# Whole-row merges in generic slots, and a later start of the first layer's second modulation

## The chip, the cores and the metric

The kernel runs on one core of a Trainium2 chip. A core has five engines that run side by side, each its instructions in order: PE (TensorE, matrix products into PSUM), DVE (VectorE), ACT (ScalarE), POOL (GpSimd) and SP (SyncE), which here issues nearly all DMA transfers. The metric is the device time of one launch in microseconds (us). Times of before: 2560.27, 2557.42 and 2563.41, median 2560.27.

## The reference

Two layers of a hybrid block over 512 tokens of x and 256 of ctx, 1024 features, in fp32. Layer 0 updates both; layer 1 only x, so it works on 512 columns where layer 0 works on 768.

```python
sh1, sc1, g1, sh2, sc2, g2 = split(silu(c) @ w_mod[l] + b_mod[l], 6)   # "modulation", from c and from c_ctx
u = x * (1 + sc1) + sh1
a, qkv, o_pre, g_if, cq, ckv, kr, gates = split(u @ w_in + b_in)
y_a = silu(layer_norm(depthwise_conv31(val * sigmoid(gate)))) @ w_conv_out
y_b = (sigmoid(o_pre) * head_norm(bidirectional_mlstm(...))) @ w_ml_out
y_c = softmax_attention(...) @ w_mla_out
g_a, g_b, g_c = split(sigmoid(gates), 3)
y = (g_a * y_a + g_b * y_b + g_c * y_c) @ w_out + b_out          # the merge
x = layer_norm(alpha * x + g1 * y)
x = layer_norm(alpha * x + g2 * (relu(u2 @ w1 + b1)**2 @ w2 + b2))
```

## The kernel before, in words

Everything is kept with features on the 128 partitions and tokens along the free axis. A feature tile of layer 0 is 128x768 (512 tokens of x, then 256 of ctx), one of layer 1 uses 512 columns of it. fp32 precision comes from splitting each operand into a high and a low part: every product is three matmuls (L266 hi by hi, L267, L268), and each weight block of 128x1024 is loaded as `wr` (L258, 512 KB), cast to `wh` on ACT (L261) and subtracted to `wl` on DVE or POOL (L262). There are three buffers each of wr, wh and wl, and `wget` loads LOOK = 2 blocks ahead. So a load of wr waits until the subtraction of the block three before it is done, and the cast into wh waits for the last matmul that reads the block three before it.

A scheduler places the instructions: from the program's order, priorities and pools it makes one fixed order per engine. All DMAs that matter stand in one order on SP. If a transfer there waits for something, all behind it wait too.

The stages of a layer that the change touches, in order:

- The modulation. The shares that are needed first (sh1, sc1) are made at the start. The others, two parts r of four groups each in layer 0, come from the generator `mod_pieces`: for each group eight loads `wm` (L160, 256 KB), each multiplied on DVE into two running sums `mda` (L163 for the first, L165 for the others), then eight small matmuls that gather the sums (L173), a copy on ACT (L176), a transpose (L178) and an addition of the bias on DVE (L181). `pull(k)` takes k steps of that generator; a step is one wm with its two operations. 64 steps make all of it. In layer 1 these pulls find nothing left.
- The 24 gates (`gate`, L760): three rows b of eight tiles mt; a gemm of 48 matmuls in layer 0, tanh on ACT, and a store of the tile to `z_dram` (L779). Behind gate 10 the convolution's normalization runs (`ln_fm` with `conv_emit`: L314 to L336, L770 to L774). Each gate pulls 2. Then four output gates `ot` (L791), also with `pull(2)`.
- `ht` (L816 to L819, then a split into `hth` on ACT, L272, and `htl` on DVE, L273): the mLSTM's heads, input of the second merge.
- `merge(b, ...)` for b = 0 (w_co, the convolution) and b = 1 (w_mo, the mLSTM): eight gemms `ps` of four k-blocks each, two for each weight block. For each gemm the row z_dram[b, mt] is loaded back as `ml` (L76), multiplied with the result on DVE (L803), for b = 1 added to the row of b = 0 on POOL (L806), and stored again (L807). PSUM has two buffers `pg` for gemms, so the third gemm needs the first one's L803.
- The last merge (L1057 on, w_ao): the same with two rows loaded (L1065, L1066 on DVE), whose result is split into `zp` (cast on ACT, L1067, subtraction on DVE, L1068) as input of w_out.

Before, a row of 768 columns is handled in pieces: 512 + 256 in the first two merges, three times 256 (two in layer 1) in the last, each piece an `ml` tile of 128x512 out of the pool "m", whose eight buffers it shares with wm, mda, th, y, xr and others. The pool "gen" has 35 slots of 128x768 for everything else.

Of the kernel before, what the change touches and what calls it, by code (L numbers as in the profile page):

```python
# [9 lines left out]
F32 = mybir.dt.float32  # L10
F32R = mybir.dt.float32r
AF = mybir.ActivationFunctionType
OP = mybir.AluOpType
# [31 lines left out]
def build(tc, I, out):  # L45
    nc = tc.nc
# [1 line left out]
    ctx = ExitStack()  # L48
    cp = ctx.enter_context(tc.tile_pool(name="const", bufs=1))
    wp = ctx.enter_context(tc.tile_pool(name="w", bufs=3))  # L50
    gp = ctx.enter_context(tc.tile_pool(name="gen", bufs=35))
    vp = ctx.enter_context(tc.tile_pool(name="v", bufs=12))
    mp = ctx.enter_context(tc.tile_pool(name="mw", bufs=8))
    sp = ctx.enter_context(tc.tile_pool(name="small", bufs=6))
# [17 lines left out]

    def mload(src):
        n = src.shape[1]
        t = mp.tile([128, 512], F32, name="ml", tag="m")
        nc.sync.dma_start(t[:, :n], src)  # L76
        return t[:, :n]

# [200 lines left out]
    def gemm(w, koff, nk, act, spec):  # L279


        ps = pg()
        if isinstance(spec, int):
            spec = [(0, 512, 0), (512, spec, 512)][:1 + (spec > 512)]
        for c0, c1, o in spec:
            for k in range(nk):
                a, b = (koff + k) * 128, (koff + k + 1) * 128
                mark[0] = mm3(ps[:, o:o + c1 - c0], w[0][:, a:b], w[1][:, a:b], act[k][0][:, c0:c1],
                              act[k][1][:, c0:c1], k == 0, k == nk - 1)
        return ps  # L290
# [55 lines left out]
    def pull(k):  # L346
        for _ in range(k):
            next(mods, None)
# [104 lines left out]
    for l in range(L):  # L453
# [322 lines left out]
        for b in range(3):  # L776
            for mt in range(8):
                g = gate(b, mt)
                nc.sync.dma_start(z_dram[b, mt, :, :n], g[:, :n])  # L779
                some_taps(3)  # L780
                pull(2)
                if b * 8 + mt == 10:
                    some_taps(200)
                    ln_fm(ca, 4, groups, conv_emit)
# [3 lines left out]
        for h in range(MH):  # L788
            ps = win(MT_O + h, n)
            t = slot("ot")  # L790
            A.activation(t[:, :n], ps[:, :n], AF.Tanh, bias=HB(MT_O + h), scale=0.5)  # L791
            ot.append(t)
            pull(2)

        def merge(b, wname, act):
            for mp2 in range(4):
                w = wget(wname, l, mp2)
                for i in range(2):
                    mt = 2 * mp2 + i
                    ps = gemm(w, 4 * i, 4, act, n)  # L800
                    for c0, c1 in segs:
                        g = mload(z_dram[b, mt, :, c0:c1])
                        V.scalar_tensor_tensor(g, g, 1.0, ps[:, c0:c1], op0=OP.add, op1=OP.mult)  # L803
                        if b:
                            z0 = mload(z_dram[b - 1, mt, :, c0:c1])
                            G.tensor_tensor(g, g, z0, op=OP.add)  # L806
                        nc.sync.dma_start(z_dram[b, mt, :, c0:c1], g)  # L807
                    pull(2)


# [246 lines left out]
        for mp2 in range(4):  # L1057
            w = wget("w_ao", l, mp2)
            for i in range(2):
                mt = 2 * mp2 + i  # L1060
                ps = gemm(w, 4 * i, 4, oT, n)
                for (_, _, c0, c1), zz in zip(tg_, zg):
                    g = mload(z_dram[2, mt, :, c0:c1])
                    z0 = mload(z_dram[1, mt, :, c0:c1])
                    V.scalar_tensor_tensor(g, g, 1.0, ps[:, c0:c1], op0=OP.add, op1=OP.mult)  # L1065
                    V.tensor_tensor(g, g, z0, op=OP.add)  # L1066
                    A.copy(zz[mt][0], g)  # L1067
                    V.tensor_sub(zz[mt][1], g, zz[mt][0])  # L1068

        parts = [(0, 0, S), (1, S, T)][:len(groups)]  # L1070
        acc = [None] * 8
# [222 lines left out]
```

## Time and profile before

| | |
|---|---|
| median of three runs | 2560.27 us |
| profiled execution: its own time | 2557.35 us |
| its span | 2555.5 us, 1.85 outside of it |
| mean granted TensorE clock | 0.993 |
| SP issues `ml<-z_dram` | 104 of 128 KB (2.8 us to landing), 48 of 256 KB (4.4 us) |
| `z_dram<-ml` | 32 of 256 KB (4.5 us) and smaller |
| `wm<-w_mod` | 192 of 256 KB (4.5 us) |

A profile's page has the busy time of each engine, the chain of work that ended last, and groups of instructions by line; the trace gives each instruction's start. A window's row gives for a stretch of the span the busy time of each engine with its instructions in brackets, the granted clock, the DMA engines' share and what they moved. A row of the timeline is start, duration, engine, line, operation, tiles, and in square brackets the idle time before it with what ended it. "SPq" rows are DMA issues.

### The profile page before, as it was taken

The numbers are of one execution on the slowest core, as the hardware profiler recorded it, in microseconds if no ns is written. First come the engines' busy times: TensorE is split into PE (matmuls) and PEld (weight loads), VectorE is DVE, ScalarE is ACT, GpSimd is POOL, SyncE is SP. The second block draws the span as 40 slices with busy tenths as digits, with TensorE's granted clock in tenths as the row PEclk, the third lists the DMA queues.
The fourth block names the chain that finished last, engine by engine and source line by source line (L and its number), as shares of the span: only waits on it lengthen the run. The fifth ranks groups of instructions, "written<-read, shape, count | busy, mean of one in ns | idle before, by whom it ended". The sixth has DMA issues, their size and how long they took to land.

```text
span 2555.5 us, 38339 instructions
## 1 busy us (share of the span) xinstructions
PE 2470.4 (97%) x15272; PEld 2163.8 (85%) x15272; DVE 1580.6 (62%) x2847; ACT 939.5 (37%) x1607; POOL 298.7 (12%) x235
## 2 busy tenths in 40 slices
PE   7899989999999999999999999999999999999997
PEld 5888878888888899888888888977888888888887
DVE  4999976363356777655554379996043567554456
ACT  3123323222457563222222253333324575432323
POOL 0002132203000021000000031023411001100002
PEclk9999999999999999999999999999999999999999
DMA  7122344466110654343342252233563106333333
GB/s 264 53 75 70 98 163 161 166 195 210 62 34 1 188 168 142 122 131 115 108 129 88 65 149 78 59 106 101 175 203 111 50 18 213 101 99 92 99 94 113
DMA packets 137235, 298.45 MB, mean 117 GB/s; under 512 B 13776, under 2 KB 55248, under 8 KB 137056
## 3 DMA queue, kind: packets, MB, share of 16 engines
q1 hardware_dynamic: 137056, 296.00, 36.9%
q8 instruction: 120, 1.97, 0.3%
q14 instruction: 59, 0.48, 0.1%
HBM read 265.49 MB, written 30.46 MB: 116 GB/s over the span
## 4 chain that ended last, share of the span: by engine, by line
PE 81%; DVE 9%; DMA 4%; ACT 2%; issue 2%; POOL 1%; SPq 0%; DVEq 0%; ACTq 0%; POOLq 0%
PE pg L266 21%; PE pg L267 21%; PE pg L268 21%; PE pt L1003 2%; PE pt L982 2%; PE pt L266 2%; PE pt L267 2%; PE pt L268 2%; DVE ca L494 2%; DMA wm<-w_mod 1%; DMA ml<-z_dram 1%; PE pg L536 1%; PE pg L538 1%; PE pg L537 1%; DVE st L315 1%
## 5 line engine op out<-in xcount | busy, mean ns | idle before, releaser
L261 ACT CAST wh<-wr 128x1024 fp32r<-128x1024 f32 (+1 forms) x328 | 345.6, 1055 | 1202.4 <-PE pg L267 825.5
L262 DVE TENSOR_TENSOR wl<-wr,wh 128x1024 fp32r<-128x1024 f32 (+2 forms) x272 | 338.6, 1246 | 410.1 <-ACT wh L261 406.3
L268 PE MATMUL pg<-uh,wl 128*128 128x512 f32 (+1 forms) x1280 | 456.3, 356 | 2.2 <-DVE wl L262 2.2
L266 PE MATMUL pg<-uh,wh 128*128 128x512 f32 (+1 forms) x1280 | 457.2, 357 | 1.2 <-ACT gt__17278 L760 1.2
L267 PE MATMUL pg<-ul,wh 128*128 128x512 f32 (+1 forms) x1280 | 455.5, 356 | 0.7 <-POOL ul L1171 0.6
L266 PE MATMUL pg<-hidh,wh 128*128 128x512 f32 (+1 forms) x832 | 285.4, 344 | 3.9 <-DVE mv L318 2.0
L267 PE MATMUL pg<-hidl,wh 128*128 128x512 f32 (+1 forms) x832 | 284.9, 342 | 0.0
L268 PE MATMUL pg<-hidh,wl 128*128 128x512 f32 (+1 forms) x832 | 284.2, 342 | 0.0
L266 PEld LDWEIGHTS pg<-uh,wh 128*128 128x128 f32 x1280 | 244.2, 191 | 35.4 <-issue 2.5
L268 PEld LDWEIGHTS pg<-uh,wl 128*128 128x128 f32 x1280 | 243.9, 191 | 34.4 <-DVE wl L262 2.7
L267 PEld LDWEIGHTS pg<-ul,wh 128*128 128x128 f32 x1280 | 244.1, 191 | 33.2 <-POOL ul L1171 1.0
L494 DVE SCALAR_TENSOR_TENSOR ca<-hc,cols,ca 128x511 f32<-128x511 f32 (+9 forms) x360 | 227.8, 673 | 2.4
L262 POOL TENSOR_TENSOR wl<-wr,wh 128x1024 fp32r<-128x1024 f32 x56 | 145.7, 2602 | 562.6 <-ACT wh L261 562.6
L267 PE MATMUL pg<-u2l,wh 128*128 128x512 f32 (+1 forms) x608 | 210.3, 347 | 0.3 <-POOL u2l L1082 0.2
L1139 DVE SCALAR_TENSOR_TENSOR acc<-pg,mod,acc 128x512 f32<-128x512 f32 (+1 forms) x168 | 106.0, 659 | 168.6 <-PE pg L268 168.6
L268 PE MATMUL pg<-u2h,wl 128*128 128x512 f32 (+1 forms) x608 | 210.1, 347 | 0.0
L266 PE MATMUL pg<-u2h,wh 128*128 128x512 f32 (+1 forms) x608 | 209.9, 347 | 0.0
L165 DVE SCALAR_TENSOR_TENSOR mda<-wm,sil,mda 128x512 f32<-128x512 f32 x224 | 176.2, 808 | 7.6 <-DMA wm<-w_mod 5.0
L266 PEld LDWEIGHTS pg<-hidh,wh 128*128 128x128 f32 x832 | 157.3, 190 | 25.3 <-issue 3.5
L321 POOL TENSOR_TENSOR rs<-rs,mhalf 128x1 f32<-128x1 f32 x30 | 24.4, 819 | 1298.5 <-DVE rs L320 1298.5
L267 PEld LDWEIGHTS pg<-hidl,wh 128*128 128x128 f32 x832 | 157.9, 190 | 18.7 <-DVE hidl L1129 1.6
L268 PEld LDWEIGHTS pg<-hidh,wl 128*128 128x128 f32 x832 | 157.7, 189 | 18.0
(359 smaller groups left out, 4754.1 us busy)
## 6 DMA issues: line engine op xcount, KB each, us to landing
wr<-w SPq DMA_DIRECT2D x140, 512.0 KB, 3.6
wr<-w_in_fm SPq DMA_DIRECT2D x104, 512.0 KB, 3.8
wm<-w_mod SPq DMA_DIRECT2D x192, 256.0 KB, 4.5
wr<-w_out SPq DMA_DIRECT2D x40, 512.0 KB, 3.9
ml<-z_dram SPq DMA_DIRECT2D x104, 128.0 KB, 2.8
ml<-z_dram SPq DMA_DIRECT2D x48, 256.0 KB, 4.4
z_dram<-ml SPq DMA_DIRECT2D x32, 256.0 KB, 4.5
dm<-m_dram SPq DMA_DIRECT2D x20, 256.0 KB, 4.4
```

The source lines that it names most:

```text
L165: ins = V.scalar_tensor_tensor(av[v], w, sil[:, k, v:v + 1], av[v], op0=OP.mult, op1=OP.add)
L261: A.copy(h[:, :n], r[:, :n])
L262: eng.tensor_sub(lo[:, :n], r[:, :n], h[:, :n])
L266: PE.matmul(ps, hs, xh, start=first, stop=False)
L267: PE.matmul(ps, hs, xl, start=False, stop=False)
L268: return PE.matmul(ps, ls, xh, start=False, stop=last)
L315: V.bn_stats(st[:, hf * 6:(hf + 1) * 6], ps)
L494: V.scalar_tensor_tensor(acc[:, a:b], h[:, a + d:b + d], wd(15 + d), acc[:, a:b], op0=OP.mult, op1=OP.add)
L536: PE.matmul(o, uh[:, t0:t0 + 128], wh[:, a:b], start=(k == 0), stop=False)
L982: PE.transpose(p2[:, y * 128:(y + 1) * 128], P[:, (k4 + y) * 128:(k4 + y + 1) * 128], ident)
L1003: PE.matmul(po[64 * i:64 * i + 64, :256], va[B_.k0 + k][:, h * 64:h * 64 + 64], B_.pts[i][k // 2][:, k % 2, :], start=(k == 0), stop=(k == ...
L1139: V.scalar_tensor_tensor(acc[mt][:, c0:c1], ps[:, c0:c1], mc[:, 40 + mt, v:v + 1], acc[mt][:, c0:c1], op0=OP.mult, op1=OP.add)
```

## The change

Four things. `mload` takes a generic slot of 128x768 instead of a tile of pool "m", and there are 40 such slots for 35; `dynamic_dma_scratch_size=1024` frees the room. The merges load, multiply, add and store whole rows; only the cast and subtraction of the last merge (now L1067 and L1068 behind L1064 and L1065) still go by groups. Gates 0 to 7 pull nothing, the others 3 steps, and so do the output gates.

```diff
--- before.py
+++ after.py
@@ -48,7 +48,7 @@
     ctx = ExitStack()
     cp = ctx.enter_context(tc.tile_pool(name="const", bufs=1))
     wp = ctx.enter_context(tc.tile_pool(name="w", bufs=3))
-    gp = ctx.enter_context(tc.tile_pool(name="gen", bufs=35))
+    gp = ctx.enter_context(tc.tile_pool(name="gen", bufs=40))
     vp = ctx.enter_context(tc.tile_pool(name="v", bufs=12))
     mp = ctx.enter_context(tc.tile_pool(name="mw", bufs=8))
     sp = ctx.enter_context(tc.tile_pool(name="small", bufs=6))
@@ -72,7 +72,7 @@
 
     def mload(src):
         n = src.shape[1]
-        t = mp.tile([128, 512], F32, name="ml", tag="m")
+        t = slot("ml")
         nc.sync.dma_start(t[:, :n], src)
         return t[:, :n]
 
@@ -778,7 +778,8 @@
                 g = gate(b, mt)
                 nc.sync.dma_start(z_dram[b, mt, :, :n], g[:, :n])
                 some_taps(3)
-                pull(2)
+                if b:
+                    pull(3)
                 if b * 8 + mt == 10:
                     some_taps(200)
                     ln_fm(ca, 4, groups, conv_emit)
@@ -790,7 +791,7 @@
             t = slot("ot")
             A.activation(t[:, :n], ps[:, :n], AF.Tanh, bias=HB(MT_O + h), scale=0.5)
             ot.append(t)
-            pull(2)
+            pull(3)
 
         def merge(b, wname, act):
             for mp2 in range(4):
@@ -798,13 +799,12 @@
                 for i in range(2):
                     mt = 2 * mp2 + i
                     ps = gemm(w, 4 * i, 4, act, n)
-                    for c0, c1 in segs:
-                        g = mload(z_dram[b, mt, :, c0:c1])
-                        V.scalar_tensor_tensor(g, g, 1.0, ps[:, c0:c1], op0=OP.add, op1=OP.mult)
-                        if b:
-                            z0 = mload(z_dram[b - 1, mt, :, c0:c1])
-                            G.tensor_tensor(g, g, z0, op=OP.add)
-                        nc.sync.dma_start(z_dram[b, mt, :, c0:c1], g)
+                    g = mload(z_dram[b, mt, :, :n])
+                    V.scalar_tensor_tensor(g, g, 1.0, ps[:, :n], op0=OP.add, op1=OP.mult)
+                    if b:
+                        z0 = mload(z_dram[b - 1, mt, :, :n])
+                        G.tensor_tensor(g, g, z0, op=OP.add)
+                    nc.sync.dma_start(z_dram[b, mt, :, :n], g)
                     pull(2)
 
 
@@ -1059,13 +1059,13 @@
             for i in range(2):
                 mt = 2 * mp2 + i
                 ps = gemm(w, 4 * i, 4, oT, n)
+                g = mload(z_dram[2, mt, :, :n])
+                z0 = mload(z_dram[1, mt, :, :n])
+                V.scalar_tensor_tensor(g, g, 1.0, ps[:, :n], op0=OP.add, op1=OP.mult)
+                V.tensor_tensor(g, g, z0, op=OP.add)
                 for (_, _, c0, c1), zz in zip(tg_, zg):
-                    g = mload(z_dram[2, mt, :, c0:c1])
-                    z0 = mload(z_dram[1, mt, :, c0:c1])
-                    V.scalar_tensor_tensor(g, g, 1.0, ps[:, c0:c1], op0=OP.add, op1=OP.mult)
-                    V.tensor_tensor(g, g, z0, op=OP.add)
-                    A.copy(zz[mt][0], g)
-                    V.tensor_sub(zz[mt][1], g, zz[mt][0])
+                    A.copy(zz[mt][0], g[:, c0:c1])
+                    V.tensor_sub(zz[mt][1], g[:, c0:c1], zz[mt][0])
 
         parts = [(0, 0, S), (1, S, T)][:len(groups)]
         acc = [None] * 8
@@ -1284,7 +1284,7 @@
     from concourse.bass_utils import run_bass_kernel_spmd
 
     arrays = pack(inputs)
-    nc = bacc.Bacc("TRN2", target_bir_lowering=False, num_devices=1)
+    nc = bacc.Bacc("TRN2", target_bir_lowering=False, num_devices=1, dynamic_dma_scratch_size=1024)
     aps = {k: nc.dram_tensor(k, v.shape, F32, kind="ExternalInput").ap() for k, v in arrays.items()}
     out = nc.dram_tensor("out", (S, D), F32, kind="ExternalOutput").ap()
     with tile.TileContext(nc) as tc:
```

The order changes at three places that matter below. Names carry a running number; the same tile has other numbers before and now.

TensorE in layer 0's gates, where the first modulation group is gathered. Before, this stands eight matmuls into gate pg_3241:

```order
L268 MATMUL pg_3241<-uh_178,wl_3094 128x512
L266 MATMUL pg_3241<-uh_264,wh_3093 128x512
L267 MATMUL pg_3241<-ul_265,wh_3093 128x512
L173 MATMUL pt_3067<-mda_2777,pick_86 32x128 [waits DVE_49]
L173 MATMUL pt_3067<-mda_2777,pick_86 32x128 x3
L268 MATMUL pg_3241<-uh_264,wl_3094 128x512
L173 MATMUL pt_3067<-mda_2778,pick_86 32x128 [waits DVE_49]
L173 MATMUL pt_3067<-mda_2778,pick_86 32x128 x3
L266 MATMUL pg_3241<-uh_272,wh_3093 128x512
```

Now the first group stands in gate pg_3645, four gates later, just ahead of the convolution's normalization (L314):

```order
L268 MATMUL pg_3645<-uh_178,wl_3300 128x512
L266 MATMUL pg_3645<-uh_264,wh_3299 128x512
L267 MATMUL pg_3645<-ul_265,wh_3299 128x512
L173 MATMUL pt_3433<-mda_3283,pick_86 32x128 [waits DVE_49]
L173 MATMUL pt_3433<-mda_3283,pick_86 32x128 x3
L173 MATMUL pt_3433<-mda_3284,pick_86 32x128 x4
L268 MATMUL pg_3645<-uh_264,wl_3300 128x512
L266 MATMUL pg_3645<-uh_272,wh_3299 128x512
L178 MATMUL pt_3444<-cst_78,modrows_3442 128x128 [waits Activation_49]
L314 MATMUL pt_3454<-cst_78,ca_606 128x128
```

The group's sums and their wait are the same; 192 matmuls of gates 7 to 10 now stand ahead of them.

SP in layer 1, where the rows of the first merge are loaded. Before, among the gates' stores and weights (w_in_fm), long ahead of the weights w_co and w_mo:

```order
L258 DMA wr_17383<-w_in_fm 128x1024 [waits DMAHW6_49,DMAHW1_49,Pool_49]
L76 DMA ml_17888<-z_dram_104 128x512 [waits DVE_49,PE_49]
L76 DMA ml_17905<-z_dram_104 128x512 [waits DMAHW0_49,DVE_49]
L76 DMA ml_17928<-z_dram_104 128x512 [waits DVE_49,PE_49]
L76 DMA ml_17945<-z_dram_104 128x512 [waits DMAHW2_49,DVE_49,PE_49]
L76 DMA ml_17968<-z_dram_104 128x512 [waits DMAHW3_49,DVE_49]
L779 DMA z_dram_104<-gt__17278 128x512 [waits DMAHW4_49,Activation_49]
L779 DMA z_dram_104<-gt__17312 128x512 [waits DMAHW5_49,Activation_49]
```

Now behind the third w_mo block, at the merge itself:

```order
L258 DMA wr_17725<-w_co 128x1024 [waits DMAHW5_49,DVE_49]
L258 DMA wr_17765<-w_mo 128x1024 [waits DMAHW7_49,DMAHW2_49,DVE_49]
L258 DMA wr_17805<-w_mo 128x1024 [waits DMAHW0_49,DVE_49]
L258 DMA wr_17845<-w_mo 128x1024 [waits DMAHW4_49,DMAHW1_49,DVE_49]
L76 DMA ml_17704<-z_dram_104 128x512 [waits PE_49]
L76 DMA ml_17721<-z_dram_104 128x512 [waits DMAHW6_49]
L76 DMA ml_17744<-z_dram_104 128x512 [waits PE_49]
L76 DMA ml_17761<-z_dram_104 128x512 [waits DVE_49]
L76 DMA ml_17784<-z_dram_104 128x512 [waits DVE_49]
L807 DMA z_dram_104<-ml_17704 128x512 [waits DMAHW5_49,DMAHW2_49,DVE_49]
```

wr_17845 waits for DVE, for the subtraction wl_17728 of the last w_co block, whose buffer it takes. The row loads moved behind it. In layer 0 the rows ml_5016 and on stand behind the third w_mo block in the same way. VectorE of layer 1 there, before:

```order
L262 TENSOR_TENSOR wl_17872<-wr_17869,wh_17871 128x1024 [waits DMAHW0_49,PE_49,Activation_49]
L819 TENSOR_SCALAR ht_17821<-ht_17821,cols1_83 128x512 [waits DVE_49]
L803 SCALAR_TENSOR_TENSOR ml_17888<-ml_17888,pg_17875 128x512 [waits PE_49]
L273 TENSOR_TENSOR htl_17830<-ht_17821,hth_17829 128x512 [waits DMAHW6_49,Activation_49]
L818 SCALAR_TENSOR_TENSOR ht_17833<-ot_17753,pt_17834 128x512
L819 TENSOR_SCALAR ht_17833<-ht_17833,cols1_83 128x512 [waits DVE_49]
L803 SCALAR_TENSOR_TENSOR ml_17905<-ml_17905,pg_17892 128x512 [waits PE_49]
L262 TENSOR_TENSOR wl_17912<-wr_17909,wh_17911 128x1024 [waits DMAHW1_49,Activation_49]
L273 TENSOR_TENSOR htl_17842<-ht_17833,hth_17841 128x512 [waits DMAHW4_49,Activation_49]
```

And now:

```order
L262 TENSOR_TENSOR wl_17728<-wr_17725,wh_17727 128x1024 [waits DMAHW1_49,PE_49,Activation_49]
L273 TENSOR_TENSOR htl_17658<-ht_17649,hth_17657 128x512 [waits DMAHW2_49,Activation_49]
L818 SCALAR_TENSOR_TENSOR ht_17661<-ot_17602,pt_17662 128x512 [waits DMAHW4_49]
L819 TENSOR_SCALAR ht_17661<-ht_17661,cols1_83 128x512 [waits DVE_49]
L273 TENSOR_TENSOR htl_17670<-ht_17661,hth_17669 128x512 [waits Activation_49]
L818 SCALAR_TENSOR_TENSOR ht_17673<-ot_17635,pt_17674 128x512 [waits DMAHW2_49]
L819 TENSOR_SCALAR ht_17673<-ht_17673,cols1_83 128x512 [waits DVE_49]
L273 TENSOR_TENSOR htl_17682<-ht_17673,hth_17681 128x512 [waits DMAHW6_49,Activation_49]
L803 SCALAR_TENSOR_TENSOR ml_17704<-ml_17704,pg_17691 128x512 [waits DMAHW5_49]
L803 SCALAR_TENSOR_TENSOR ml_17721<-ml_17721,pg_17708 128x512 [waits DMAHW6_49]
```

All of ht now stands ahead of the first L803 (ml_17704).

SP in layer 1's last merge, before, round one of its w_out loads:

```order
L76 DMA ml_20278<-z_dram_104 128x256 [waits DMAHW5_49,DVE_49]
L76 DMA ml_20284<-z_dram_104 128x256 [waits DMAHW4_49,DVE_49]
L76 DMA ml_20286<-z_dram_104 128x256 [waits DVE_49]
L76 DMA ml_20305<-z_dram_104 128x256 [waits DMAHW7_49,DMAHW6_49,DVE_49]
L76 DMA ml_20307<-z_dram_104 128x256 [waits DMAHW1_49,DVE_49]
L258 DMA wr_20469<-w_out 128x1024 [waits DMAHW0_49,DVE_49]
L76 DMA ml_20313<-z_dram_104 128x256 [waits DVE_49]
L76 DMA ml_20315<-z_dram_104 128x256 [waits DMAHW2_49,DVE_49]
```

And now:

```order
L76 DMA ml_20051<-z_dram_104 128x512 [waits DMAHW4_49]
L76 DMA ml_20053<-z_dram_104 128x512 [waits DMAHW5_49]
L258 DMA wr_20237<-w_out 128x1024 [waits DMAHW6_49,DVE_49]
L76 DMA ml_20080<-z_dram_104 128x512 [waits DMAHW7_49]
L76 DMA ml_20082<-z_dram_104 128x512 [waits DMAHW0_49]
L76 DMA ml_20103<-z_dram_104 128x512 [waits DMAHW1_49]
L76 DMA ml_20105<-z_dram_104 128x512 [waits DMAHW2_49]
L258 DMA wr_20269<-w_out 128x1024 [waits DMAHW3_49,DVE_49]
L76 DMA ml_20132<-z_dram_104 128x512 [waits DMAHW4_49]
L76 DMA ml_20134<-z_dram_104 128x512 [waits DMAHW5_49]
L258 DMA wr_20301<-w_out 128x1024 [waits DMAHW6_49,DVE_49]
L76 DMA ml_20155<-z_dram_104 128x512 [waits DMAHW7_49]
```

Before, seven pairs of pieces stand ahead of that w_out load, wr_20469, the first of three; now four row loads, those of mt 0 and 1, stand ahead of the first of them, wr_20237, and those of mt 2 and 3 (ml_20080 to ml_20105), of mt 4, and of mt 5 to 7 follow one w_out load each. Each of these waits for DVE, for a subtraction.

## The prediction

> **What bounds the kernel now.** I read the page first: the busy shares, and the chain of waits that ended last.
>
> ```profile
> PE 2470.4 (97%) x15272; PEld 2163.8 (85%) x15272; DVE 1580.6 (62%) x2847; ACT 939.5 (37%) x1607; POOL 298.7 (12%) x235
> PE 81%; DVE 9%; DMA 4%; ACT 2%; issue 2%; POOL 1%; SPq 0%; DVEq 0%; ACTq 0%; POOLq 0%
> L165 DVE SCALAR_TENSOR_TENSOR mda<-wm,sil,mda 128x512 f32<-128x512 f32 x224 | 176.2, 808 | 7.6 <-DMA wm<-w_mod 5.0
> ```
>
> TensorE carries the time, so an edit matters only where TensorE stops. Next I took windows round the places that the change touches (after the length: PE busy, weight loads, DVE, ACT, POOL, granted clock, DMA share, GB/s), what TensorE waited for there, and the chain from 300 to 420.
>
> ```profile
> 320.00:330.00 10.00, 9.36 (x53) 7.89 (x51) 8.18 (x20) 2.84 (x4) 6.10 (x4) 1.00 0.48 150
> 330.00:340.00 10.00, 2.66 (x19) 1.37 (x20) 9.12 (x15) 0.27 (x1) 0.99 (x1) 0.72 0.57 177
> 340.00:350.00 10.00, 10.00 (x55) 8.63 (x54) 9.29 (x16) 1.85 (x2) 2.11 (x1) 0.94 0.63 207
> ...
> 600.00:610.00 10.00, 8.09 (x43) 6.79 (x42) 4.32 (x7) 0.00 (x0) 6.23 (x5) 1.00 0.87 268
> 1670.00:1680.00 10.00, 5.98 (x26) 5.04 (x25) 9.04 (x11) 1.06 (x2) 2.37 (x1) 0.83 0.43 125
> 1880.00:1890.00 10.00, 10.00 (x46) 8.29 (x45) 8.06 (x13) 3.11 (x4) 0.00 (x0) 1.00 0.74 238
> ```
> ```profile
> PE pt L173 <- DVE mda L165: 8.0, 1, 8.0
> ```
> ```profile
> PE pg L266 <- DVE ml L803: 3.6, 2, 1.9
> PE pt L173 <- DVE mda L165: 0.6, 1, 0.6
> ```
> ```profile
> PE pg L266 <- DVE ml L1065: 1.4, 2, 1.2
> ```
> ```profile
> 328.44 2.89 DVE hacc L748 x3
> ...
> 337.34 0.65 PE pt L173 x8
> 337.99 0.73 PE pg L268
> 338.72 0.58 PE pt L173 x8
> 339.31 0.72 PE pg L266
> ...
> 355.14 0.57 PE pt L173 x16
> ...
> 373.91 2.85 DVE mda L165
> ```
>
> The wait rows (total, times, longest) are of 320 to 345, of 540 to 612 (layer 0's merges) and of 2104 to 2140 (layer 1's w_ao merge). At 329 TensorE reaches the transposes of the first modulation group (L173), while VectorE still has that group's sums behind the normalization (L748): a stop of 8.0 us. In layer 1's first merge (1880 to 1890) TensorE never stops.
>
> **What the change gains.** (1) Gates 0 to 7 pull nothing, so the first group's transposes stand four gates later, behind 192 more matmuls, which are four gates of 8.3 us, 33 us in all. Its last five weight loads now stand on SP behind the store of gate 8, which by gates of 8.3 us ends at 345 (the wait at 329 is eight matmuls into gate 7). The first lands 4.4 us on (256 KB, row below), the others 0.98 apart at the 268 GB/s of 600 to 610, and six sums of 0.81 follow the last: 359. TensorE comes to the transposes at 329 + 33 = 362. So the 8.0 us go, and the slow stretch behind them: 0.65 + 0.73 + 0.58 + 0.72 = 2.68 us for what takes 0.57 (16 transposes at 355) and two matmuls of 0.23, so 1.65 too much, and some 0.5 at clock 0.94. That is 10.1; I leave 0.1 for what stays: **-10.0** (between 0, if the wait moves along, and -10.6). What hides the sums then is gate matmuls; without that cover they cost the 8.0 again.
> (2) The sum at 373.91 stood ahead of the conv normalization's statistics, 2.85 us; in the new order none stands there: **-2.4**, the part that TensorE stopped (0 to -2.9). The later groups come 17 to 25 us apart and need 14 x 0.81 = 11.3 us of VectorE: hidden. The one behind the normalization waits about 2 us now and then: 0.
> (3) VectorE loses 63 instructions and SP 88 issues. Covered by TensorE's matmuls, since VectorE is 62% busy: 0. The scratch setting and the five slots issue nothing: 0.
>
> **What it costs: row loads come to stand behind weight loads on SP.** Layer 1's first merge, as it runs now, has the durations:
>
> ```profile
> 1878.35 1.05 ACT L261 CAST wh<-wr 128x1024 fp32r<-128x1024 f32 x1 [2.08 <-PE pg L267]
> ...
> 1882.89 0.62 ACT L272 CAST hth<-ht 128x512 fp32r<-128x512 f32 x1 [2.96 <-DVE ht L819]
> ```
> ```profile
> 1879.43 1.23 DVE L262 TENSOR_TENSOR wl<-wr,wh 128x1024 fp32r<-128x1024 f32 x1 [0.22 <-ACT wh L261]
> 1880.58 0.69 DVE L273 TENSOR_TENSOR htl<-ht,hth 128x512 fp32r<-128x512 f32 x1
> 1881.18 0.68 DVE L818 SCALAR_TENSOR_TENSOR ht<-ot,pt 128x512 f32<-128x512 f32 x1
> 1881.78 0.68 DVE L803 SCALAR_TENSOR_TENSOR ml<-ml,pg 128x512 f32<-128x512 f32 x1
> 1882.38 0.48 DVE L819 TENSOR_SCALAR ht<-ht,cols 128x512 f32<-128x512 f32 x1
> ...
> 1894.85 0.69 DVE L803 SCALAR_TENSOR_TENSOR ml<-ml,pg 128x512 f32<-128x512 f32 x1 [2.03 <-PE pg L268]
> ```
> ```profile
> 571.17 1.02 DVE L803 SCALAR_TENSOR_TENSOR ml<-ml,pg 128x512 f32<-128x512 f32 x2 [3.16 <-PE pg L268]
> ```
> ```profile
> 1786.65 2.54 SPq L76 DMA_DIRECT2D ml<-z_dram  x5
> ...
> 1880.69 0.33 SPq L258 DMA_DIRECT2D wr<-w_mo  x1
> ```
> ```profile
> ml<-z_dram SPq DMA_DIRECT2D x104, 128.0 KB, 2.8
> ml<-z_dram SPq DMA_DIRECT2D x48, 256.0 KB, 4.4
> ```
>
> A gemm takes 2.03 + 0.69 = 2.7 us in layer 1 and 3.16 + 1.02 = 4.2 in layer 0. Today the rows are loaded from 1786 on, some 90 us early. In the new order they stand behind the w_mo load of 1880.69. That one waits until the subtraction of 1879.43 has freed its slot, and the cast ahead of it waits for the end of the second gemm (1878.35). So the first row is issued at 1881.1 and lands at about 1885 (4 us; 4.4 by the group). VectorE's order also puts every L818, L819 and L273 ahead of the first L803: from 1880.6 on, 0.6 each from start to start, L273, L818, L819, the cast on ACT, L273, L818, L819, the cast, L273, to 1885.9, then L803 to 1886.6. The third gemm needs the PSUM buffer that this L803 frees (there are two), and TensorE is in order. It stands from 1878.4 to 1886.6: **+8.2** (4, if only the load counts; 9, if it lands late).
>
> Layer 0's first merge has the same order with rows of 768 columns. I take 0.95 us for an operation on a whole row, since its two parts take 1.02 at 571. After the second gemm: cast 1.05, subtraction 1.15, then L273 0.9, L818 0.95, small ones and L819 1.15, cast 0.85, L273 0.95, L803 0.95, together 7.95; TensorE has 0.7 of transposes meanwhile. With a little waiting for the load, 7.5. The 3.6 + 0.6 = 4.2 us of the wait rows go, 1.9 of them in the second merge, whose rows are then loaded five gemms ahead: **+3.3** (0 to +6).
>
> The merges of w_ao (L1057 on), layer 1 as it runs now:
>
> ```profile
> 2102.13 9.29 SPq L76 DMA_DIRECT2D ml<-z_dram  x10
> 2112.09 0.33 SPq L258 DMA_DIRECT2D wr<-w_out  x1
> ...
> 2117.06 0.33 SPq L258 DMA_DIRECT2D wr<-w_out  x1
> ...
> 2124.16 0.33 SPq L258 DMA_DIRECT2D wr<-w_out  x1
> ```
> ```profile
> 2109.28 1.06 ACT L261 CAST wh<-wr 128x1024 fp32r<-128x1024 f32 x1 [0.63 <-PE pg L267]
> ```
> ```profile
> 2126.13 0.28 PE L266 MATMUL pg<-zp,wh 128*128 128x256 f32 x1
> ```
>
> Now each w_out load finds the next rows already issued. Then rows 0 and 1 stand ahead of the first of these loads, rows 2 and 3 behind it, row 4 behind the second, rows 5 to 7 behind the third (rows and gemms numbered from 0). Gemm 1 ends at 2109.4; cast and subtraction to 2111.6; row 2 issued 2112, landed 2116. But the next subtraction waits for gemm 3 (2115.6, then 1.05 + 1.2) and stands ahead of row 2's L1064: 2118.4, so gemm 4 waits 2.9 us. The third load waits for the subtraction behind gemm 5 (2123.9, so 2126.1); row 5 lands 4.2 later, its L1064 ends at 2131.1, and gemm 7 waits 4.4 us. It ends at 2133.8 instead of 2126.1, 7.7 late; the 1.4 us of waits that the w_out gemms have now come off, since row 7 is then ready in time: **+6.3** (3 to 9). Layer 0 by the same steps:
>
> ```profile
> 870.15 0.90 DVE L1065 SCALAR_TENSOR_TENSOR ml<-ml,pg 128x256 f32<-128x256 f32 x2 [0.51 <-PE pg L268]
> ```
>
> Gemm 5 ends at 870.1, the subtraction behind it at 872.3, row 5 lands about 5 us later (384 KB behind 512) and its L1064 of 0.95 ends at 878.3, while gemm 6 ends at 874.3: gemm 7 waits 4.0 us. The earlier gemms do not wait, since a gemm of 4.2 us covers more. At the end a subtraction, then L1064, L1065, cast and L1068 of the last row (0.95 + 0.95 + 0.4 + 0.4) follow gemm 7, some 1.1 more than the pieces take now: **+5.1** (2 to 8).
>
> **Slow clock behind long waits.** Behind the 8.0 us wait the granted clock is 0.72 and 0.94, behind one of 4 us at 1671 it is 0.83. The first case cost 1.65 + 0.5 us, small waits included; I take 1.2 for each of four new waits above 4 us: **+4.8** (0 to 7).
> [...]
>
> **Sum.** -10.0 - 2.4 + 8.2 + 3.3 + 6.3 + 5.1 + 4.8 = +15.3. The profiled execution took 2557.35 us, so 2572.7; it stands 2.9 under the median shown (2560.27), on which the sum would be 2575.6. I keep 2573.
>
> **Rivals.** A, no change: the w_ao merges stay covered, because whole rows land in 2 us rather than 4. Then -12.4 + 8.2 + 3.3 + 2.4 of clock = +1.5, 2559. Against it: those loads are issued only after the gemm before theirs has ended.
> B, faster: the row loads are never late, because SP's weight load is released one gemm earlier than I read (2.7 or 4.2 us) and VectorE's order does no harm. Then -12.4 and the old 4.2 go too: 2541. It decides at what the cast waits for: the row at 1878.35 names the matmul that ends the second gemm.
> C, much slower: the first group's wait comes back at gate 11, if its loads land some 12 us later than I count (+8 to 10); or layer 0's second merge is bound by DMA. Three rows of 384 KB and half a weight per gemm of 4.2 us are 340 GB/s; 600 to 610 moved 268. At 268 a gemm would take 5.3 us, 8 x 1.2 = +9.5. Either gives about 2583. Against the second: 18 MB in the 64 us from the first merge's loads on are 285 GB/s, and the early ones have time.
>
> **Chances.** Forecast 0.62, A 0.17, B 0.10, C 0.11. Some 0.2% (5 us) is what a measurement of this kernel can tell from no change. Slower: the forecast and C, 0.72 after rounding; same: A, 0.17; faster: B, 0.11. The range runs from below A (2556) to C (2583); B and what of C lies above are left out. The forecast's own range, by its terms' bounds partly cancelling, is 2564 to 2581.
>
> **What would show it.** Right: TensorE busy near 10 from 320 to 350; in each layer's first merge one wait of 7 to 8 us on L803, with row loads issued just behind a w_mo load; in the w_ao merges waits of 3 to 5 us on L1064; clock under 1 behind each. Wrong: no such waits, a long wait on mda at gate 11, or waits under 2 us in w_ao.

## Result and profile after

The changed kernel takes 2586.85 us (median of 4 runs, 2586.65 to 2592.31), the kernel before in the same series 2558.85 (2557.2 to 2563.41). The ratio is 1.0112, 95% interval 1.0092 to 1.0131: slower by 28 us, where 15 were forecast, and 4 above the upper end of the range. The profiled execution took 2587.0 us, its span is 2585.2.

The page of the changed kernel, busy shares, chain of waits and the group of modulation sums:

```profile
PE 2484.6 (96%) x15272; PEld 2174.5 (84%) x15272; DVE 1583.1 (61%) x2783; ACT 938.0 (36%) x1607; POOL 294.5 (11%) x227
...
PE 81%; DVE 10%; DMA 3%; ACT 2%; issue 2%; POOL 1%; SPq 0%; DVEq 0%; ACTq 0%; POOLq 0%
...
L165 DVE SCALAR_TENSOR_TENSOR mda<-wm,sil,mda 128x512 f32<-128x512 f32 x224 | 180.8, 828 | 24.0 <-DMA wm<-w_mod 21.6
```

The shares hardly tell the two kernels apart: TensorE executes the same 15272 instructions and is busy 14 us longer, at a mean granted clock of 0.986 for 0.993; the other half of the loss is waiting. One row does point to a place: VectorE's modulation sums now wait 24.0 us, 21.6 of them for their weights (7.6 and 5.0 before).

TensorE's waits in the changed kernel, place by place: 360 to 425 (the gates and the convolution's normalization), 520 to 612 (layer 0's merges), 844 to 900 (layer 0's w_ao merge), 1870 to 1915 (layer 1's first merge), 2104 to 2170 (layer 1's w_ao merge). The columns are total, times, longest, in us. From 320 to 345 there is none any more.

```profile
PE pt L173 <- DVE mda L165: 4.2, 1, 4.2
PE pt L336 <- DVE rs L322: 1.7, 1, 1.7
```
```profile
PE pg L266 <- DVE ml L803: 5.3, 1, 5.3
PE pt L173 <- DVE mda L165: 1.6, 1, 1.6
```
```profile
PE pg L266 <- DVE ml L1064: 5.2, 2, 4.1
```
```profile
PE pg L266 <- DVE ml L803: 8.4, 1, 8.4
```
```profile
PE pg L266 <- DVE ml L1064: 8.8, 4, 5.0
```

Each forecast wait is there, and one above 2 us that was not forecast: 4.2 us at 402, for the second modulation group. (The 1.6 us on `mda` in layer 0's merges belong to the stretch of the 5.3: the group's transposes stand just ahead of the third gemm.) Windows of the changed kernel (length; busy of PE, weight loads, DVE, ACT, POOL; granted clock; DMA share, GB/s):

```profile
340.00:350.00 10.00, 10.00 (x61) 8.88 (x60) 5.62 (x5) 1.85 (x2) 2.85 (x1) 1.00 0.64 216
...
400.00:410.00 10.00, 5.82 (x41) 4.39 (x40) 8.02 (x13) 0.27 (x1) 0.00 (x0) 0.75 0.64 203
540.00:550.00 10.00, 5.71 (x21) 4.74 (x21) 4.15 (x9) 0.83 (x1) 0.00 (x0) 0.66 0.95 338
...
1890.00:1900.00 10.00, 4.98 (x12) 3.92 (x13) 4.15 (x7) 1.23 (x2) 0.00 (x0) 0.50 0.89 309
```

In and behind each of these three stops the mean granted clock is down: 0.75, 0.66, 0.50. The chain through the stop of layer 1's first merge (start, us, what) shows how the row loads and L803 get there:

```profile
1886.16 0.24 PE pg L267
...
1886.47 1.05 ACT wh L261
...
1887.55 1.24 DVE wl L262
...
1888.80 0.33 SPq L258
...
1889.18 0.42 SPq L76
...
1889.65 4.00 DMA ml<-z_dram
...
1893.67 0.69 DVE htl L273
1894.37 0.61 DVE ml L803
...
1895.02 0.79 PE pg L266
1895.81 0.43 PE pg L267
```

The second gemm ends; only then can ACT cast the weight, VectorE subtract, SP issue the w_mo load that stood ahead of the row loads, and the rows come in. The DMA row of the chain is not what ended the wait, though: it starts at 1889.65, so it is the second row's load. The first row, issued at 1889.18, had landed by 1892.99 (the last of its 16 semaphore updates in the trace), and its L803 began only at 1894.28. VectorE was still at the rest of ht, which stands ahead of L803 in its order; the last L273 started when ACT's cast for it ended at 1893.64:

```profile
1893.02 0.62 ACT L272 CAST hth<-ht 128x512 fp32r<-128x512 f32 x1 [1.88 <-DVE ht L819]
```

Elsewhere it is the load: in layer 0's first merge the row landed at 543.17 and L803 began at 543.19, and the long stop of each w_ao merge ends the same way (877.55 and 877.57, 2152.11 and 2152.13). The 2.8 us stop in layer 1's w_ao merge, at 2137.80, has no load in its chain: a subtraction of 1.22 us (L262) ahead of L1064 ended it. The last row of the chain above is the other part of the price: 0.43 us for a matmul that took 0.24 before the stop.

To compare kernels by place I add up TensorE's loss: for each matmul or transpose, the time to the next start less the median of that for its line, output tile and shape in the same trace, in us (sums to about 0.1). Kernels of the experiments stand beside it (their edits are below); "w_ao, layer 1" runs to the end, since the slower kernels are shifted there.

| place (us) | before | after | pulls | rows | own | slots | early4 |
|---|---|---|---|---|---|---|---|
| gates, 300 to 430 | 20.3 | 14.4 | 14.4 | 22.8 | 14.4 | 22.8 | 12.3 |
| layer 0's merges, 500 to 640 | 8.1 | 11.9 | 9.2 | 15.5 | 2.4 | 15.6 | 2.2 |
| w_ao, layer 0, 830 to 930 | 4.8 | 13.2 | 4.7 | 11.1 | 4.4 | 27.4 | 3.3 |
| layer 1's first merges, 1860 to 1950 | 0.2 | 11.0 | 0.2 | 10.8 | 0.5 | 10.8 | 1.4 |
| w_ao, layer 1, from 2085 | 9.7 | 20.2 | 8.9 | 20.0 | 7.5 | 33.9 | 7.3 |
| elsewhere | 94.5 | 95.9 | 93.8 | 92.1 | 98.1 | 93.6 | 96.4 |
| sum | 137.6 | 166.6 | 131.2 | 172.3 | 127.3 | 204.1 | 122.9 |

The change gains 5.9 us in the gates and loses 33.5 in the four merges (3.8 + 8.4 + 10.8 + 10.5); elsewhere 1.4. That is the 29.0 by which the sums differ.

### The profile page after: what moved, and what is told of

Its sections match the earlier page's. It is cut to its first block, busy times and chain, and to the rows that moved or that the text cites. A ratio compares the mean times of both kernels' runs of the same rounds, so it can differ in the third digit from the quotient of the medians.

```text
span 2585.2 us, 38052 instructions
## 1 busy us (share of the span) xinstructions
PE 2484.6 (96%) x15272; PEld 2174.5 (84%) x15272; DVE 1583.1 (61%) x2783; ACT 938.0 (36%) x1607; POOL 294.5 (11%) x227
## 4 chain that ended last, share of the span: by engine, by line
PE 81%; DVE 10%; DMA 3%; ACT 2%; issue 2%; POOL 1%; SPq 0%; DVEq 0%; ACTq 0%; POOLq 0%
PE pg L266 21%; PE pg L267 21%; PE pg L268 21%; DVE ca L494 3%; PE pt L1003 2%; PE pt L982 2%; PE pt L266 2%; PE pt L267 2%; PE pt L268 2%; DVE wl L262 1%; DMA wm<-w_mod 1%; DMA ml<-z_dram 1%; ACT wh L261 1%; PE pt L336 1%; DVE st L315 1%
## 5 line engine op out<-in xcount | busy, mean ns | idle before, releaser
L262 DVE TENSOR_TENSOR wl<-wr,wh 128x1024 fp32r<-128x1024 f32 (+2 forms) x272 | 338.9, 1247 | 422.7 <-ACT wh L261 418.9
L268 PE MATMUL pg<-uh,wl 128*128 128x512 f32 (+1 forms) x1280 | 456.2, 356 | 2.3 <-DVE wl L262 2.3
L268 PE MATMUL pg<-hidh,wl 128*128 128x512 f32 (+1 forms) x832 | 283.8, 341 | 0.0
L268 PEld LDWEIGHTS pg<-uh,wl 128*128 128x128 f32 x1280 | 244.4, 191 | 34.8 <-DVE wl L262 2.7
L268 PE MATMUL pg<-u2h,wl 128*128 128x512 f32 (+1 forms) x608 | 209.8, 346 | 0.0
L262 POOL TENSOR_TENSOR wl<-wr,wh 128x1024 fp32r<-128x1024 f32 x56 | 141.9, 2533 | 568.9 <-ACT wh L261 556.2
L165 DVE SCALAR_TENSOR_TENSOR mda<-wm,sil,mda 128x512 f32<-128x512 f32 x224 | 180.8, 828 | 24.0 <-DMA wm<-w_mod 21.6
L268 PEld LDWEIGHTS pg<-hidh,wl 128*128 128x128 f32 x832 | 157.4, 189 | 18.0
```

Of the source, the lines that this page charges most:

```text
L165: ins = V.scalar_tensor_tensor(av[v], w, sil[:, k, v:v + 1], av[v], op0=OP.mult, op1=OP.add)
L262: eng.tensor_sub(lo[:, :n], r[:, :n], h[:, :n])
L268: return PE.matmul(ps, ls, xh, start=False, stop=last)
```

## Experiments

The theory (Q): it is not the whole rows that cost, but where a shared slot puts their loads. A pool hands out its slots in the order of the program. In the kernel before, the rows had tiles of another pool and could be loaded long ahead; with generic slots a row load can only stand on SP behind the loads that lead to the tiles ahead of it (ot, ht, zp), and so behind weight loads that wait; the operation that uses the row comes later in VectorE's order too. The rivals: the whole rows themselves (W: larger transfers, longer operations), and the pulls (P).

**pulls** and **rows**: each half of the change alone. Pulls takes the kernel before and edits two places; rows takes the changed kernel and undoes them.

```diff
                 some_taps(3)
-                pull(2)
+                if b:
+                    pull(3)
...
             ot.append(t)
-            pull(2)
+            pull(3)
```

> The kernel before with only the pulls of the change (gates 0 to 7 pull nothing, the later gates and the tanh gates three each); merges in pieces from their own pool. Theory Q (the loss is row loads that share the generic slots and so come to stand on SP behind weight loads that wait): none of the four merge waits, so the window 320 to 420 alone counts. There the two profiles lose 19.3 us before and 12.75 after, so about 6.6 us under before, 2552, with a wait of some 4.2 us on mda at the second modulation group (402 us) still in it, since its weight loads stand behind a waiting w_in_fm load here too. Rival P (the pulls are to blame for the waits in layer 0's merges, since 14 modulation sums now fall there): some 3 us of waits stay at 535 to 540, and the gain is 3 us or less, 2556.

> The changed kernel with the pulls of before: whole rows in 40 generic slots alone. Theory Q: the four merge regions lose what they lose in the changed kernel against before (3.5 in layer 0's first merge, 8.5 and 10.5 in the two w_ao merges, 11.0 in layer 1's first merge, 33.5 in all), and the first modulation group's wait of 8 us at 329 stays: 2559 + 33.5 = 2592. If the pulls made the merges worse (rival P), less than that: 2580 to 2586.

Measured: pulls 2551.4 us, ratio 0.9979 (0.9970 to 0.9987); rows 2593.01 us, 1.0137 (1.0122 to 1.0153). The halves have opposite signs, and they nearly add: -5.2 and +36.4 give 31, the two together 28. Pulls' waits, 320 to 430 and 500 to 620:

```profile
PE pt L173 <- DVE mda L165: 4.2, 1, 4.2
```
```profile
PE pg L266 <- DVE ml L804: 3.4, 2, 2.0
```

So the 4.2 us at 402 comes with the pulls alone, and layer 0's merges keep about the waits of before (3.4 for 3.6). Rows, 520 to 612 (L803 is L802 there):

```profile
PE pg L266 <- DVE ml L802: 10.9, 1, 10.9
```

Against rival P, this is longer than the changed kernel's 5.3: the pulls do not make the merges worse.

**slots**: the kernel before, its pieces and pulls kept, but each piece takes a generic slot. This gives the pool without the whole rows.

```diff
-    gp = ctx.enter_context(tc.tile_pool(name="gen", bufs=35))
+    gp = ctx.enter_context(tc.tile_pool(name="gen", bufs=40))
...
-        t = mp.tile([128, 512], F32, name="ml", tag="m")
+        t = slot("ml")
...
-    nc = bacc.Bacc("TRN2", target_bir_lowering=False, num_devices=1)
+    nc = bacc.Bacc("TRN2", target_bir_lowering=False, num_devices=1, dynamic_dma_scratch_size=1024)
```

> The kernel before, merges in pieces and its own pulls, with one thing changed: the pieces take a generic slot (40 of them, and the scratch setting of the changed kernel) in place of a tile of their own pool. Theory Q: in layer 1 a piece is the whole row of 512 tokens, SP's and VectorE's order is that of the changed kernel, so its 8.4 us wait on L803 and the slow matmuls behind it come (11 us); the w_ao merges wait as in the changed kernel or somewhat less (12 to 19 us in both layers), layer 0's first merge 2 to 6: 2559 + 25 to 36 = 2584 to 2595. Rival W (whole rows cost it): as before, 2557 to 2562.

Measured: 2629.71 us, 1.0284 (1.0267 to 1.0301). Rival W falls: without one whole row more than in the kernel before, the waits come. Layer 1's first merge, where a piece is a whole row of 512 tokens anyway, has the 8.4 us wait and the loss of 10.8. But it costs 73 us, twice what I expected, and the miss is in w_ao. TensorE's waits there, layer 0 (844 to 915) and layer 1 (2090 to 2215):

```profile
PE pg L266 <- DVE ml L1065: 16.8, 5, 6.7
```
```profile
PE pg L266 <- DVE ml L1065: 13.5, 6, 3.9
```

A row there is three pieces in layer 0 and two in layer 1, each for two operands, and each now takes a slot of its own; that this is why it waits more is argued and not shown. In generic slots whole rows are the cheaper form: rows has the same slots and pulls and takes 2593.01.

**own**: the other corner: the changed kernel with whole rows and its pulls, but the rows in a pool of their own.

```diff
-    gp = ctx.enter_context(tc.tile_pool(name="gen", bufs=40))
+    gp = ctx.enter_context(tc.tile_pool(name="gen", bufs=35))
     vp = ctx.enter_context(tc.tile_pool(name="v", bufs=12))
+    rp = ctx.enter_context(tc.tile_pool(name="row", bufs=5))
...
-        t = slot("ml")
+        t = rp.tile([128, T], F32, name="ml", tag="r")
```

> The changed kernel, whole rows as before it, but the row tiles come from a pool of their own (5 buffers of 128 x 768), generic slots back at 35. Theory Q: the first rows of each first merge are again issued among the gates, five row tiles stand ahead of the w_out loads, and VectorE's L803 stands between the L818 again. So no wait on L803 above 2 us in layer 1 and none of 5 us in layer 0, w_ao waits of at most 2 us: 2559 - 6.6 for the gates - up to 3 for layer 0's old waits + 0 to 4 for w_ao, 2550 to 2556. Rival W (the whole rows themselves cost it: transfers of 384 KB that land in 5.9 us instead of 2.8 to 4.4, VectorE operations of 0.95 us, buffers that come free later): the waits stay where they are in the changed kernel, 2575 to 2587.

Measured: 2548.08 us, 0.9965 (0.9952 to 0.9977), faster than before and 2 us under the range that I expected; its profiled execution took the same. No wait on a row is left in any merge. The chain of own and its two waits from 320 to 430 (its lines stand one later):

```profile
PE 86%; DVE 8%; ACT 2%; DMA 2%; issue 1%; POOL 1%; SPq 0%; DVEq 0%; ACTq 0%; POOLq 0%
```
```profile
PE pt L174 <- DVE mda L166: 3.5, 1, 3.5
PE pt L337 <- DVE rs L323: 2.1, 1, 2.1
```

**early4**: a pool of one's own might help only because 40 generic slots come free too late. So here the rows stay in the 40 generic slots, and only the place in the program at which they are taken moves: four rows ahead in the merges, three in w_ao.

```diff
...
+        def fetch(k):
+            for _ in range(k):
+                if todo_r:
+                    b, mt = todo_r.pop(0)
+                    rows[b, mt] = [mload(z_dram[b, mt, :, :n])]
+        fetch(4)
         ot = []
...
-                    g = mload(z_dram[b, mt, :, :n])
+                    g = rows.pop((b, mt))[0]
...
                     nc.sync.dma_start(z_dram[b, mt, :, :n], g)
+                    fetch(1)
...
+        fetch_a(3)
         zg = []
...
-                g = mload(z_dram[2, mt, :, :n])
-                z0 = mload(z_dram[1, mt, :, :n])
+                g, z0 = rows_a.pop(mt)
...
+                fetch_a(1)
```

> The changed kernel (whole rows in the 40 generic slots, its pulls), with the rows' slots taken earlier in the program: four rows ahead in the two merges (the first four before the tanh gates), three rows of both operands ahead in the w_ao merge. Theory Q1 (what costs the time is when the program takes the slot, since that sets the place of the load on SP and of L803 on VectorE): layer 1's first merge has no wait above 2 us on L803, layer 0's none of 5 us, w_ao under half of its waits; of the 28 us lost against before at least 20 come back: 2553 to 2566. Rival Q2 (the generic slots are too few or come free too late, whatever the order in which they are taken): the rows taken early push other tiles back, the waits stay or move, 2575 to 2590.

Measured: 2544.86 us, 0.9950 (0.9938 to 0.9963). Q1 holds, and 42 us come back, more than the loss and 8 us beyond the expected range. Row loads of early4 in layer 1 on SP, and the one wait that its first merges (1860 to 1930) have left (L803 is L813 there):

```profile
1836.74 0.38 SPq L76 DMA_DIRECT2D ml<-z_dram  x1
1840.29 1.35 SPq L76 DMA_DIRECT2D ml<-z_dram  x3
```
```profile
PE pg L266 <- DVE ml L813: 0.6, 1, 0.6
```

The first four rows are asked for some 20 us ahead of the merge, whose first matmul starts at 1859.95; the changed kernel's merge starts at 1881.01, and it asks at 1889.18, in the middle of it. Early4 moves the load and L803 together, so it doesn't tell how much each is worth alone.

**pieces**: does own gain by whole rows or by the pool? Pieces in a pool of their own, with the change's pulls.

```diff
+    rp = ctx.enter_context(tc.tile_pool(name="row", bufs=7))
...
-        t = mp.tile([128, 512], F32, name="ml", tag="m")
+        t = rp.tile([128, 512], F32, name="ml", tag="r")
```

(The scratch setting is that of the changed kernel.)

> The kernel before with the change's pulls, merges in pieces, and the pieces in a pool of their own (7 buffers of 128 x 512, apart from the modulation's tiles). It tells whether the row pool's kernel gains by whole rows or by the pool. Whole rows (fewer operations: 0.95 us against two parts of 1.02 us in sum, fewer issues): the two waits on L803 in layer 0 stay (3.4 us, as with the pulls alone) and the 1.2 us in w_ao of layer 1, 2550 to 2553. The pool: those waits go here too, 2546 to 2549.

Measured: 2555.2 us, 0.9992 (0.9983 to 1.0001). By the forecast's first case, and 2 us worse: pieces keeps waits on the rows, 2.2 us in layer 0's merges, 1.5 in layer 0's w_ao and 1.6 in layer 1's w_ao.

Loaded in time, whole rows are a gain: the losses in layer 0's merges and the two w_ao merges are 2.4 + 4.4 + 7.5 = 14.3 us in own, and 6.3 + 6.7 + 10.0 = 23.0 in pieces. Seven pieces hold less than five rows (3584 against 3840 columns), so a small part of that may be depth. The pool alone gave the pieces nothing: with the same pulls and the pool of before they took 2551.4 (pulls).

**gapC** and **gapE**: the wait at 402. Its chain in the changed kernel:

```profile
388.05 2.43 POOL wl L262
...
390.50 0.33 SPq L258
...
390.92 0.38 SPq L160
...
391.40 5.65 DMA wm<-w_mod
...
405.17 1.41 DVE mda L165 x2
...
406.62 0.66 PE pt L173 x8
```

The second group's first weights stand on SP behind a w_in_fm load, which waits for POOL's subtraction of 2.43 us; the first lands by 394.8, the second at 397, and the sums that the transposes need end at 406.6, 4.2 us after TensorE has come to their transposes. GapC gives the group more time (its transposes come 4 us later); gapE puts its loads ahead of the waiting one. Both start from own.

```diff
-                    pull(3)
+                    pull(1 if b * 8 + mt in (11, 12) else 3)    # gapC
+                    pull(7 if b * 8 + mt == 10 else 2 if b * 8 + mt in (11, 12, 13, 14) else 3)    # gapE
```

> The kernel with the rows' own pool, and at gates 11 and 12 one pull in place of three, so that the second modulation group's transposes stand some 20 matmuls later and its weight loads stand where they stood. There the row pool's kernel waits 3.5 us on mda at about 402 us and loses 14.4 us between 300 and 430. If the loads only come too late for that place: the wait falls to about 0 to 1 us, the slow matmuls behind it go, 3 to 5 us less, 2543 to 2546. If the wait moves along (the loads stand behind the conv normalization's VectorE work or wait for tiles of the small pool): no change, 2547 to 2550, with a wait on mda at a later place.

> The kernel with the rows' own pool, and gate 10 pulls seven in place of three (gates 11 to 14 two each), so that the second group's weight loads stand on SP ahead of the w_in_fm load that waits some 10 us for its slot; its transposes come about 20 matmuls earlier. If that waiting load is what makes the group late: no wait on mda at 400, 3 to 6 us less than the row pool's kernel, 2542 to 2545. If VectorE is what makes it late (the group's sums now stand among the conv normalization's statistics): the wait on the normalization (2.1 us at 390) grows by 3 us or more and the time stays at 2547 to 2551.

Measured: gapC 2550.05 us, 0.9970 (0.9959 to 0.9980); gapE 2545.37 us, 0.9952 (0.9939 to 0.9964); own, in another series, 0.9965. Their waits from 365 to 430, gapC and then gapE:

```profile
PE pt L174 <- DVE mda L166: 3.9, 1, 3.9
PE pt L337 <- DVE rs L323: 2.1, 1, 2.1
```
```profile
PE pt L337 <- ACT ln L327: 3.7, 2, 1.9
PE pg L267 <- ACT gt__3713 L761: 2.3, 1, 2.3
```

In gapC the wait moves along with the transposes, though the window loses 11.4 in place of 14.4 us; layer 0's merges give 3.1 of it back (5.5 against 2.4). In gapE four of the group's eight weights are loaded ahead of the waiting load (359.55 to 365.53), and the wait on mda is gone, though the transposes come earlier. So what the group lacked was its weights in time. But shorter waits on ACT take its place, and the window loses 12.7. From own to gapE the intervals overlap: that gapE is faster is not shown.

**best**: early4 with gapE's pulls.

> The two edits that were faster than before, together: whole rows in generic slots that are taken early (2544.9 us, 0.9950 of before) and gate 10 pulling seven, gates 11 to 14 two each (it took 14.4 to 12.7 us off the loss between 300 and 430 in the row pool's kernel). In the early rows' kernel that window loses 12.3 us, 2.9 of it the second group's wait on mda. If the edits add: the wait goes, 1 to 3 us less, 2542 to 2544, a ratio of 0.994. If the second edit only trades the wait for others (3.7 us on the normalization and 2.3 on a gate's tanh in the row pool's kernel): 2544 to 2548, no change against the early rows alone.

Measured: 2545.16 us, 0.9949 (0.9937 to 0.9962); its loss from 300 to 430 is 12.5 us, early4's 12.3. The second case: the pulls trade one wait for others. Early4, best and gapE are the fastest measured, and no run tells them apart: all about 0.5% under the kernel before and about 40 us under the changed kernel.

## Why the prediction was right in sign and short in size

**Right.** The direction, and the mechanism of all four merge waits. TensorE came to the first group's transposes at 362.2 us, as forecast, and their last sum had ended at 360.0. By the wait rows, but for the first line:

| step | forecast | measured |
|---|---|---|
| first modulation group at 329, wait and slow stretch | -10.0 | -11.6 (loss from 320 to 360: 11.6, now 0.0) |
| layer 1's first merge | +8.2 | +8.4 |
| layer 0's merges | +3.3 | 5.3 + 1.6 - 4.2 = +2.7 |
| w_ao, layer 1 | +6.3 | 8.8 - 1.4 = +7.4 |
| w_ao, layer 0 | +5.1 | +5.2 |

These merge waits sum to 23.7 us where 22.9 were forecast. The chain at 1886 has the links of the forecast in its order (cast, subtraction, weight load, row load), and VectorE's order is what set the length there, as forecast: by the load alone L803 could have begun at 1892.99, 1.3 us earlier. Of the rivals, A needed the w_ao waits to stay away, B the row loads to be in time and VectorE's order to do no harm, C the first group's wait to come back at gate 11 or a merge bound by DMA; the second merge of layer 0 has no wait on a row. None happened.

**What failed: step (2), "The one behind the normalization waits about 2 us now and then: 0".** I had counted VectorE's 11.3 us against the 17 to 25 us between groups, and not asked from when they run. The group's weights are asked for at 390.92, behind the load that waits for POOL, so its 11 us of sums start at 394.8 and do not fit ahead of 402. The stretch from 400 to 430 loses 8.3 us where it lost 2.8: +5.4 for a term of 0. It was the same mechanism as in the merges, a load behind a waiting weight load on SP, and I did not look for it there; pulls shows the wait without the whole rows, gapE takes it away by moving the load.

**Step (2) failed in its other term too, -2.4 for the sum at 373.91.** TensorE's waits on the normalization in the kernel before, 320 to 430 (the changed kernel has one of 1.7 us, in the view further up):

```profile
PE pt L336 <- ACT ln L326: 3.8, 3, 2.2
```

The 2.2 us stop at 379 did go, as forecast. But the normalization's second part now stops TensorE for 1.7 us at 383.7, and slow matmuls follow:

```profile
380.00:390.00 10.00, 8.28 (x45) 7.36 (x44) 5.71 (x15) 6.55 (x12) 3.05 (x3) 0.83 0.21 82
```

The stretch from 360 to 400 loses 5.1 us where it lost 4.9: nothing gained. In all, the gates gained 5.9 us in place of 12.4: -11.6 + 0.3 + 5.4 for -10.0 - 2.4 + 0. That is 6.5 of the miss.

**What was mis-sized: the slow clock, "1.2 for each of four new waits", +4.8.** The merges lose 33.5 us more than before, their waits 23.7 more, so 9.8 are slow matmuls and small gaps: twice the term. Behind the 8.56 us stop of layer 1's first merge the next 6.5 us hold 2.5 us of it, behind a stop of 5.6 in layer 0's merges 2.0, behind one of 4.25 in layer 0's w_ao 1.7, and layer 1's w_ao has two such stops (2.9 and 5.1 us, with 1.8 and 1.6) where I counted one: 9.6 in all. (A stop counts here from start to start, less the median; that is some 0.2 us more than the idle time of a wait row.) The stop at 329 had shown 1.65 + 0.5 us, and I cut it to 1.2 on the guess that small waits made the rest; and I counted stops above 4 us only, where five stops had it, one of them of 2.9 us.

The miss by place (29.0 - 15.3 = 13.7): 6.5 from the gates, 5.0 from the clock, 0.8 from the waits, 1.4 elsewhere. The forecast's own range ended at 2581 because I let the terms' bounds partly cancel, and the whole range at rival C's 2583; the terms that missed went the same way.

## To carry to other kernels

A tile that moves into a shared pool takes its place in the order of allocation, and its load takes that place in the DMA queue with it, as the operation that uses it does in its engine's order: own and early4 differ from the changed kernel only in the pool that the rows' tiles come from, or in the place of the program at which they are taken, and run about 40 us faster. Before such a move, look on the queue for what the load now stands behind and what that waits for, and on the engine for what the operation now stands behind; and if the slots are to be shared, take them as many steps ahead as the load used to run. Where a group of work is delayed, check where its first load then stands, not only whether its total fits; and price each stop of the bounding engine with the slow stretch behind it (here 1.6 to 2.5 us in the 6.5 us behind each of five stops of 2.9 to 8.6 us).

## What the runs showed of the hardware

Slow matmuls follow stops that are shorter than I had thought, and not each time. Five stops stand at the same place in all eleven traces (before, after and the nine experiments), each with less than 0.1 us lost in the 5 us ahead of it. The loss is that of the 6.5 us behind the stop:

| stop, in front of (line of before, us) | its length (us) | traces in which the next 6.5 us lose more than 1 us | their loss (us) | loss in the others |
|---|---|---|---|---|
| L898, 666 to 687 | 1.6 | 3 of 11 (after, gapC, own) | 1.7, 1.7, 2.6 | 0.2 |
| L268, 173 to 176 | 2.4 | 10 of 11 | 1.6 to 1.8 | 0.1 |
| L694, 258 to 261 | 2.7 | 9 of 11 | 1.7 to 1.8 | 0.1 to 0.2 |
| L725 in layer 1, 1662 to 1708 | 4.2 | 11 of 11 | 1.6 to 2.8 | |
| L536, 112 to 114 | 7.0 | 11 of 11 | 1.3 to 2.7 | |

The stop of 8.6 us in layer 1's first merge was followed by 2.3 to 2.5 us in all three kernels that have it. The five microseconds behind the 1.6 us stop, before and after:

```profile
678.00:683.00 5.00, 5.00 (x28) 4.35 (x29) 1.55 (x3) 2.66 (x4) 1.33 (x1) 1.00 0.35 121
```
```profile
676.00:681.00 5.00, 4.88 (x22) 4.17 (x23) 1.77 (x3) 2.17 (x4) 1.33 (x1) 0.72 0.35 121
```

The same work, the granted clock 1.00 in the one and 0.72 in the other. What decides below 3 us no run here settles; kernels that differ by less than about 2 us can differ by this alone (an estimate from the table: behind the same short stop the traces differ by 1.5 to 2.4 us).
